# A two-layer diffusion trunk: another clock for the order of the instructions, and part of the modulation on quarters of TensorE's columns

## The chip, the cores and the metric

One core of a Trainium2 chip runs the whole step. The metric is device time in microseconds. The engines are TensorE (PE, with its weight loads PEld), VectorE (DVE), ScalarE (ACT), GpSimd (POOL) and SyncE (SP), which issues the DMAs. All five work through their own instructions in order and wait for each other by semaphores.

## The reference

The trunk has two layers on 128 context tokens and 512 latent tokens of 1024 features. The first mixes by gated linear attention and retention (4 heads each), the second by latent attention (8 heads); each is followed by a squared-ReLU MLP of 4096. Around each sub-layer stand norms, and a modulation that is computed from two condition vectors, c for the latent tokens and c_ctx for the context:

```python
def ada_mod(cond, w_ada, b_ada):
    m = jnp.einsum('bd,de->be', jax.nn.silu(cond), w_ada) + b_ada
    return jnp.split(m[:, None, :], 6, axis=-1)      # shift, scale, gate, shift, scale, gate

def pre_norm_mod(x, g, shift, scale):
    return rms_norm(x, g) * (1.0 + scale) + shift

def post_norm_residual(x, y, g, gate):
    return x + gate * rms_norm(y, g)

# per layer: mixer(pre_norm_mod(x)) -> post_norm_residual, mlp(pre_norm_mod(x)) -> post_norm_residual
# within a tile the gated linear attention needs, for both directions,
#   a = where(causal, (q * exp(b)) @ (k * exp(-b)).T, 0) ; o = q_dec @ S + a @ v
```

w_ada has 1024 rows and 6 x 1024 columns for each layer, 24 MB a layer. All is float32.

## The kernel before

The 640 tokens stand in 5 tiles of 128 (tile 0 the context). Large products take both operands as two summands of a shorter float format, hi and lo, and add three products (`mm3`); ScalarE rounds the weights to hi (`wh`), DVE or POOL subtracts to get lo (`wl`). Small products keep full float32, in two passes.

The program is not written in its final order. Its parts are generators (threads); `Weave` holds a rough clock for each engine, takes each instruction's time from a table in `Engine.way`, and gives out the instructions in the order in which an engine that is free would take them, by priority and then by age. What comes out is a fixed order on each engine. Where the table is off, an engine meets an instruction whose operands are not there yet, and all behind it waits.

The modulation has 12 parts (2 layers, 6 each), each in two halves of 512 columns. A half needs 8 blocks of 128 rows of w_ada (tile `rada`). There are two ways to compute it:
- `ada_first` does shift and scale of the first norm, for which all else waits. PE multiplies each block with a 128 x 4 matrix `wide` that holds both conditions; four of the eight row blocks of scale go to DVE (`FIRST_ON_VECTOR`), whose sums PE adds by columns of ones. The bank's 4 rows are copied to `row` and turned to columns.
- `ada_half` and `ada_cols` do all other parts. DVE multiplies each block by a condition per row and adds, once for each condition (`ada<-rada,cT,ada`, 16 instructions a half), then transposes in blocks of 32 (`tr`) and reduces (`sums`); a PE product with `fold` adds the 4 groups of partitions (`pc`).

The parts of the even layer's gate and of its MLP's shift and scale (`ADA_EVEN`) run during the even layer, the rest in the MLPs. The first projection, `gemm_first`, runs the first group of columns (480) over all tiles with the first half of the features, then with the second, as the first norm's modulation comes by halves. In the even layer `tile_thread` does a tile's work, among it the scores of the two directions: 4 products of 64 rows for the forward direction into one bank, then 4 for the backward one.

Of the kernel before, what the change touches and what calls it, by code (L numbers as in the profile page):

```python
# [35 lines left out]
NCONST = 1320  # L36


def _constants():
# [4 lines left out]
    # running sums of log decays over a tile, taken from its middle (the 1/16 of the gate is in here)  # L44
# [20 lines left out]
    c[:, C_FOLD:] = j % 32 == np.arange(32)  # L65
# [4 lines left out]
# The parts of the kernel are generators that emit instructions; they are interleaved by a rough  # L70
# clock per engine, so that each engine's instructions come in the order in which their operands do.
# [5 lines left out]
class Slots:  # L77
    """The tiles of a tag (or of several pools), handed out and given back."""
# [16 lines left out]
class Weave:  # L95
    """Each thread's instructions come in their order; an engine that is free takes, of those that could start,
    the one of the lowest priority number, then the one that has waited longest (the vector engine: the
    one of the oldest thread)."""
# [14 lines left out]
    # what a thread does between two yields  # L113
    def put(self, *ways):
        """An instruction, in one way or another: engine, time, what emits it."""
        self.cur.todo.append((ways, self.beside))

    def later(self, do):
        """Something for the order itself, behind what the thread has to do so far."""
        if self.running:  # L120
            self.cur.todo.append((((None, 0.0, do),), False))
# [32 lines left out]
    # the order  # L154
# [9 lines left out]
    def _at(self, th, eng):  # L164
        """When what the thread's next instruction needs is there."""
# [6 lines left out]
    def _end(self, th, eng, us):  # L172
        """When that could be through on this engine, behind those that go first."""
# [4 lines left out]
    def _advance(self, th):  # L178
        """To the thread's next instruction, or to what it waits for."""
        while th.todo:  # L180
            ways, beside = th.todo[0]
            if ways[0][0]:
                eng, us, do = ways[0] if len(ways) == 1 else min(ways, key=lambda x: self._end(th, *x[:2]))
                th.todo[0] = us, do, beside
# [25 lines left out]
    def _issue(self, eng, start):  # L210
# [3 lines left out]
        # rather idle for a moment than be in the way of what is more urgent  # L214
# [7 lines left out]
        us, emit, beside = th.todo.popleft()  # L222
        emit()
        if eng == "SP":
# [33 lines left out]
class Engine:  # L258
    """An engine of nc whose instructions also move its rough clock."""
# [4 lines left out]
    def way(self, fn, a, k):  # L264
# [6 lines left out]
        if fn == "dma_start":  # L271
            return "SP", out.shape[0] * n * 4 / 350e3, emit
        if name == "PE":
# [10 lines left out]
            return name, us, emit  # L284
# [3 lines left out]
        psum = any(x.space == bass.MemoryType.PSUM for x in aps)  # L288
        if name == "DVE":
            fast = fn in ("tensor_copy", "tensor_scalar", "memset") and not psum  # L290
            return name, 0.07 + n / (1920 if fast else 960) + 0.06 * small, emit
        if name == "ACT":
            return name, (0.05 if psum else 0.094) + n / 1200 + 0.093 * small, emit
        return name, 0.15 + n * 2.1e-3, emit
# [3 lines left out]


class Either:  # L300
    """Whichever of some engines is through with it first."""
# [20 lines left out]
class Trunk:  # L322
# [31 lines left out]
    def at_last(self, left, do):  # L354
        """do() when the last of left[0] comes here."""
# [11 lines left out]
    def split(self, hi, lo, src, eng=None):  # L367
        """src == hi + lo, both in the tensor engine's one-pass float32 format."""
# [9 lines left out]
    def rsqrt(self, m, r, t, scale, post=1.0):  # L378
        """r = post * (scale * m) ** -0.5, with a Newton step behind exp(-ln / 2)."""
# [13 lines left out]
    def weight(self, src, shape, lo="vector", pair=False, quota=None, room=None, prio=1):  # L393
        """To be brought in as its two summands, in the order of these calls."""
# [4 lines left out]
    def weights(self):  # L399
        """Their loads; weight_rooms() finds room for the summands."""  # L400
# [64 lines left out]
    def gemm_nat(self, units, n, out, ready=None, done=None):  # L465
        """One group of columns, tile by tile of tokens: sets out[t] to the bank."""
# [20 lines left out]
    def gemm_first(self, units, n, out, ready):  # L487
        """The same, all tiles with the first half of the rows, then all with the second."""
# [25 lines left out]
    def ada_loads(self, parts, slots, nk=1, ahead=16, after=None):  # L514
        """The rows of w_ada behind ada_half(), nk * 128 at a time."""
# [16 lines left out]
    def ada_later(self, secs, slots, nk=1, ahead=16):  # L532
        """Loads of whole parts, in their order."""
        self.w.spawn(self.ada_loads([(l, sec, half, k0) for l, sec in secs for half in range(2)
                                     for k0 in range(0, KC, nk)], slots, nk, ahead, self.loaded))

    def ada_half(self, l, sec, half, rest, n=KC):
        """Partial sums over the rows' 128 features of silu(cond) @ w_ada, for both conditions."""
# [1483 lines left out]
```

## Time and profile before

| | us |
|---|---|
| median of 3 runs | 1617.75 |
| lowest, highest | 1616.5, 1625.09 |
| span of the profiled execution | 1615.8 |
| PE busy in it | 1529.0 (95%) |
| DVE, ACT, POOL busy | 1051.6, 634.0, 397.4 |
| mean granted TensorE clock | 0.977 |

The stages in the trace: the first norm and its modulation up to the first projection at 37 us, the even layer to about 410, its MLP to about 845, the latent attention to about 1160, and the second MLP to the end. An instruction shows as busy until its result is out, and those on PE overlap, so the distance of two starts tells the rate, and the busy time of one is longer. The clock of PE is granted in full or in half, in stretches of 3.4 or 6.8 us; a mean of 0.85 over a stage stands for 30% of it at half.

### The profile page before, as it was taken

The page shows a single profiled execution, that of the slowest core. Times are in us where ns is not written, and L with a number is a line of the kernel's source. Part 1 is how long each engine was busy: PE and PEld are TensorE (multiplying, and loading weights), DVE is VectorE, ACT ScalarE, POOL GpSimd, SP SyncE. Part 2 cuts the span into 40 slices and gives each one's busy share as a digit, 9 for nine tenths or more (in the row PEclk, how much of TensorE's full clock was granted, in tenths as well). Part 3 has the DMA queues.
Part 4 walks back from the last instruction along what each step waited for, and adds up shares of the span by engine and source line. Part 5 has one row for each costly group of instructions (what it writes and reads, how often), then busy time and mean ns, then how long its engine had stood idle before and what let it go on. Part 6 is the DMA issues. An engine that isn't in the chain of part 4 may idle for free. (4 is left out here: it accounts for less than half of the span.)

```text
span 1615.8 us, 22873 instructions
## 1 busy us (share of the span) xinstructions
PE 1529.0 (95%) x8583; PEld 1338.8 (83%) x8583; DVE 1051.6 (65%) x1915; ACT 634.0 (39%) x1485; POOL 397.4 (25%) x317
## 2 busy tenths in 40 slices
PE   5999988889999999999997989999899999999997
PEld 1587767777888998998896989998799989988996
DVE  5577898885577778768748788884766333333335
ACT  2473433354532322332235556664543223222332
POOL 2423644432111211211136320012212112111213
PEclk9999999999999999999998999999999999999999
DMA  8323423333265454445322301113344222222211
GB/s 307 106 64 109 121 85 114 102 117 96 73 178 163 143 147 142 137 144 150 116 61 84 97 21 27 40 40 118 104 130 130 72 74 68 90 79 66 78 53 65
DMA packets 146733, 166.12 MB, mean 103 GB/s; under 512 B 12112, under 2 KB 92480, under 8 KB 146624
## 3 DMA queue, kind: packets, MB, share of 16 engines
q1 hardware_dynamic: 146624, 164.68, 33.8%
q8 instruction: 67, 1.10, 0.3%
q14 instruction: 42, 0.34, 0.1%
HBM read 158.69 MB, written 5.96 MB: 102 GB/s over the span
## 5 line engine op out<-in xcount | busy, mean ns | idle before, releaser
L266 PE MATMUL p<-hT,wh 128*128 128x256 f32 (+1 forms) x2048 | 444.3, 309 | 0.0
L266 PE MATMUL p<-wh,hid 128*128 128x512 f32 x1280 | 401.8, 392 | 0.0
L266 PEld LDWEIGHTS p<-hT,wh 128*128 128x128 f32 x2048 | 342.6, 188 | 1.4
L266 PE MATMUL p<-hT,wl 128*128 128x256 f32 (+1 forms) x1024 | 316.6, 309 | 0.0
L266 POOL TENSOR_TENSOR r<-r 128x384 f32<-128x384 f32 (+1 forms) x128 | 133.6, 1044 | 725.8 <-ACT hid L266 725.8
L266 PEld LDWEIGHTS p<-wh,hid 128*128 128x128 f32 x1280 | 241.8, 189 | 49.2
L266 PE MATMUL pg<-wh,hT 128*128 128x512 f32 (+3 forms) x840 | 269.4, 394 | 3.9 <-ACT hT L266 3.5
L266 ACT CAST wh<-raw 128x1024 fp32r<-128x1024 f32 (+3 forms) x169 | 172.3, 1026 | 251.2 <-PE p L266 243.3
L266 PE MATMUL p<-wl,hid 128*128 128x512 f32 x640 | 251.1, 392 | 0.0
L266 DVE SCALAR_TENSOR_TENSOR ada<-rada,cT,ada 128x512 f32<-128x512 f32 x292 | 238.7, 859 | 2.6 <-DMA rada<-in_w_ada 2.4
L266 DVE TENSOR_TENSOR wl<-raw,wh 128x1024 fp32r<-128x1024 f32 x121 | 148.3, 1225 | 89.5 <-ACT wh L266 88.3
L266 PEld LDWEIGHTS p<-hT,wl 128*128 128x128 f32 x1024 | 193.4, 189 | 0.2
L266 PEld LDWEIGHTS pg<-wh,hT 128*128 128x128 f32 x840 | 158.0, 194 | 37.9 <-issue 8.1
L266 DVE TENSOR_TENSOR y<-y,p 128x512 f32<-128x512 f32 x140 | 95.9, 685 | 104.7 <-PE p L266 104.5
L266 DVE TENSOR_TENSOR hid<-r,hid 128x384 fp32r<-128x384 f32 (+1 forms) x128 | 63.9, 500 | 152.6 <-POOL r L266 152.6
L266 ACT ACTIVATE r<-p 128x384 f32<-128x384 f32 (+1 forms) x128 | 56.1, 439 | 266.5 <-PE p L266 266.3
L266 POOL TENSOR_TENSOR wl<-raw,wh 128x1024 fp32r<-128x1024 f32 (+3 forms) x44 | 105.1, 2400 | 211.1 <-ACT wh L266 184.0
L266 PE MATMUL pg<-wl,hT 128*128 128x512 f32 (+3 forms) x360 | 145.8, 405 | 1.1 <-POOL wl L266 1.1
L266 PEld LDWEIGHTS p<-wl,hid 128*128 128x128 f32 x640 | 120.9, 189 | 24.2
L266 PEld LDWEIGHTS pg<-wl,hT 128*128 128x128 f32 x360 | 70.2, 195 | 16.3 <-issue 2.6
L266 ACT ACTIVATE hid<-r 128x384 fp32r<-128x384 f32 (+1 forms) x128 | 60.4, 472 | 2.2
L266 PE MATMUL ps<-kn,qn 128*128 128x320 f32 (+1 forms) x216 | 49.7, 311 | 1.4 <-ACT prob L266 1.4
(259 smaller groups left out, 2013.8 us busy)
## 6 DMA issues: line engine op xcount, KB each, us to landing
raw<-in_w_mlp SPq DMA_DIRECT2D x128, 512.0 KB, 4.2
rada<-in_w_ada SPq DMA_DIRECT2D x160, 256.0 KB, 2.9
rada<-in_w_ada SPq DMA_DIRECT2D x16, 512.0 KB, 5.4
raw<-in_w_in_even SPq DMA_DIRECT2D x16, 512.0 KB, 3.7
x<-in_x_sample SPq DMA_DIRECT2D x8, 512.0 KB, 7.7
gate<-gate SPq DMA_DIRECT2D x8, 512.0 KB, 4.6
raw<-in_w_out_even SPq DMA_DIRECT2D x8, 512.0 KB, 3.9
raw<-in_w_out_odd SPq DMA_DIRECT2D x8, 512.0 KB, 4.2
```

The lines of the kernel that those rows point to most:

```text
L266: emit = lambda: real(*a, **k)
```

## The change

The diff also strips comments and docstrings; those lines are left out here. It has four parts.

1. The order's clock: matmul times are replaced (128 columns of a one-pass product 0.058 in place of 0.108 us, 512 columns 0.2275 in place of 0.216, small float32 products on at most 64 rows more), and a new clock "port" is held by POOL's instructions and by those of DVE that read two operands from SBUF or copy within it: while one holds it the other is not started.
2. The first norm's shift and scale are computed by PE alone. `wide` becomes a 34-column matrix with the conditions in columns 2 and 3; a slice of 32 columns of it is the stationary side. Four blocks of rows are one batch, and block j writes partitions 32 j to 32 j + 31 of the bank. All 128 rows are copied, and a product with `fold`, which is now 128 x 128, adds the four quarters while it turns them to columns.
3. The three parts of `ADA_EVEN` go the same way, two batches a half, with four buffers for their loads in place of two. DVE's accumulators move from the whole kernel's pool to the MLPs'.
4. The scores of both directions go into two banks as one batch of 8 products, the two directions in turn.

```diff
 Engine.way:
             if fn == "transpose":
-                us = 0.108
+                us = 0.08
             elif x.dtype == F32:
-                us = 2 * max(0.108, m * 2 / 2400)
+                us = 2 * max(0.113 if x.shape[0] > 64 else 0.213, m * 2 / 2400)
             else:
-                us = max(0.108, m / 2400 + 0.0025)
+                us = max(0.058, m * 0.4385e-3 + 0.003)
...
+            port = sbuf > 1 or fn in ("tensor_copy", "tensor_scalar") and not psum
...
-        return name, 0.15 + n * 2.1e-3, emit
+        return name, 0.2 + n * (0.6e-3 if fn == "memset" else 2.15e-3), emit, fn != "memset"
 Weave._issue:
+        if port:
+            start = max(start, self.clk.get("port", 0.0))
+            self.clk["port"] = start + us
 new:
+    def batch(self, fn, calls, us):
+        ways = [self.way(fn, a, k) for a, k in calls]
+        self.w.put((self.name, us, lambda: [x[2]() for x in ways], False))
+    def ada_four(self, ps, rows, start, stop):
+        self.nc.tensor.batch("matmul", [
+            ((ps[32 * j:32 * j + 32], self.wide[:, kc, 2 - 2 * sec:34 - 2 * sec], raw), dict(start=start, stop=stop))
+            for j, (raw, kc, sec) in enumerate(rows)], 1.4)
+    def ada_turned(self, ps, n, row):
+        nc.scalar.copy(row, ps)
+        yield
+        for j in range(4):
+            nc.tensor.matmul(ps[:, n * j:n * j + n], row[:, j * P:(j + 1) * P], self.fold[:, 0:n], start=True, stop=True)
+    def ada_tensor(self, l, sec, half, res):
+        ps, hp = yield from self.bank()
+        for k0 in (0, 4):
+            got, held = [], []
+            for kc in range(k0, k0 + 4):
+                raw, hr = yield self.ada_ev[l, sec, half][kc]
+                got.append((raw, kc, 0))
+                held += hr
+            self.ada_four(ps, got, k0 == 0, k0 == 4)
...
 ada:
+            if (l, sec) in ADA_EVEN:
+                yield from self.ada_tensor(l, sec, half, res)
+                continue
 ada_first:
-            n = FIRST_ON_VECTOR[half]
-                w.spawn(by_vector(half, n, done))
-                nc.tensor.matmul(ps[0:4], wide[:, sec * KC + kc], raw, start=(sec, kc) == todo[0],
+            todo = [(k0, sec) for k0 in (0, 4) for sec in (1, 0)]
+            for i, (k0, sec) in enumerate(todo):
...
+                self.ada_four(ps, got, i == 0, i == 3)
 even:
-        self.ada_later(ADA_EVEN, self.slots(ph, "erada", 2))
+        self.ada_later(ADA_EVEN, self.slots(ph, "erada", 4))
 tile_thread:
+            nc.tensor.batch("matmul", [((pas[d][0][:, c], kt[r, c], qt[r, 0, c]), dict(start=True, stop=True))
+                                       for c in cols_ for d, r in enumerate(rows_)], 2.2)
```

PE, the first norm's modulation, before and now. `rada` is a pair of row blocks, `xn` a normed tile that is turned; the first number of the size is the columns of the stationary side.

```order
L266 MATMUL ps_140<-rada_137,wide_114 4x512 x2
L266 MATMUL ps_140<-rada_149,wide_114 4x512
L266 MATMUL ps_140<-rada_146,wide_114 4x512
L266 MATMUL ps_250<-ident,xn_238 128x128
L266 MATMUL ps_140<-rada_149,wide_114 4x512
L266 MATMUL ps_250<-ident,xn_238 128x128
L266 MATMUL ps_140<-rada_146,wide_114 4x512
```

```order
L269 MATMUL ps_134<-rada_137,wide 32x512 x2
L269 MATMUL ps_134<-rada_143,wide 32x512 x2
L269 MATMUL ps_240<-ident,xn_226 128x128 x3
L269 MATMUL ps_134<-rada_140,wide 32x512 x2
L269 MATMUL ps_134<-rada_146,wide 32x512 x2
L269 MATMUL ps_240<-ident,xn_226 128x128
L269 MATMUL ps_134<-fold,row_135 128x4 x4
```

The products of four columns stood one by one between the transposes; now two rows (four products) stand together, and four small products with `fold` follow.

PE, the end of the first half of the first projection (`pg`), now: the first batch of `ADA_EVEN` stands between the halves, where before no modulation of that kind was on PE.

```order
L269 MATMUL ps_553<-ident,xn_313 128x128 x4
L269 MATMUL ps_558<-ident,xn_380 128x128 x4
L269 MATMUL ps_566<-rada_322,wide 32x512
L269 MATMUL ps_566<-rada_330,wide 32x512
L269 MATMUL ps_566<-rada_334,wide 32x512
L269 MATMUL ps_566<-rada_336,wide 32x512
L269 MATMUL pg_337<-wh_360,hT_91 128x480
```

All twelve batches now stand ahead of the first transposes of `dup`, the decayed queries and keys of the retention.

DVE, the rows ahead of the first copy to `dup`, before and now; `ga` is the gate of the linear attention, `sm` small columns of a norm.

```order
L266 SCALAR_TENSOR_TENSOR ada_1519<-rada_1736,cT,ada_1519 128x512
L266 SCALAR_TENSOR_TENSOR ada_1520<-rada_1736,cT,ada_1520 128x512
L266 TENSOR_REDUCE sm_1809<-sq_1808 128x4
L266 TENSOR_SCALAR sm_1809<-sm_1809 128x4
L266 STREAM_TRANSPOSE tr_1857<-ada_1519 128x512
L266 TENSOR_TENSOR sm_1809<-sm_1809 128x4 x2
L266 TENSOR_SCALAR sm_1809<-sm_1809 128x4
L266 TENSOR_TENSOR sm_1809<-sm_1809 128x4
L266 COPY dup_1884<-qk_1873 128x4x64
```

```order
L269 TENSOR_SCALAR sm_1802<-sm_1802 128x4
L269 SCALAR_TENSOR_TENSOR ga_1662<-ps_1752,sm_1751,ga_1662 128x128
L269 TENSOR_TENSOR sm_1766<-sm_1766 128x4
L269 TENSOR_TENSOR ga_1850<-pg_1759,ga_1850 128x512
L269 COPY dup_1905<-qk_1892 128x4x64
```

The multiply-adds and the transpose of the modulation are gone from here.

More of the change, by code (lines that the diff above doesn't have):

```diff
@@ L629, in ada_first @@
         res = [self.mod_tile(sec) for sec in range(2)]
-        wide, hd = yield from self.take(self.tmp, [P, 512], F32, "wide")
-        wide = wide[:, 0:72].rearrange("p (k c) -> p k c", c=4)
-        nc.vector.memset(wide, 0.0)
-        for c in range(2):
-            nc.vector.memset(wide[:, 16 + c, 2 + c:3 + c], 1.0)
+        nc.vector.memset(self.wide, 0.0)
         def load():
@@ L650, in load @@
             w.set(self.loaded)
-        def by_vector(half, n, done):
-            acc = yield from self.ada_half(0, 1, half, 0.0, n)
-            w.set(done, acc)
         w.spawn(load())
         yield prepared
-        for sec in range(2):
-            nc.vector.tensor_copy(wide[:, sec * KC:sec * KC + KC, sec * 2:sec * 2 + 2],
-                                  self.cT.rearrange("p (c k) -> p k c", c=2))
+        nc.vector.tensor_copy(self.wide[:, :, 2:4], self.cT.rearrange("p (c k) -> p k c", c=2))
         for half in range(2):
@@ L663, in ada_first @@
             row, hw = yield from self.take(self.tmp, [P, 512], F32, "row")
-            n = FIRST_ON_VECTOR[half]
-            done = Event()
-            if n:
-                w.spawn(by_vector(half, n, done))
-            todo = [(sec, kc) for kc in range(KC) for sec in range(2) if sec == 0 or kc >= n]
-            for sec, kc in todo:
-                raw, hr = yield self.ada_ev[0, sec, half][kc]
-                nc.tensor.matmul(ps[0:4], wide[:, sec * KC + kc], raw, start=(sec, kc) == todo[0],
-                                 stop=n == 0 and (sec, kc) == todo[-1])
-                self.drop(*hr)
-                yield
-            if n:
-                acc = yield done
-                for c in range(2):
-                    nc.tensor.matmul(ps[0:4], wide[:, 16 + c], acc[c], start=False, stop=c == 1)
-                yield
-            nc.scalar.copy(row[0:4], ps[0:4])
-            for j in range(4):
-                nc.tensor.transpose(ps[:, 4 * j:4 * j + 4], row[0:4, j * P:(j + 1) * P], self.ident[0:4, 0:4])
-            yield
+            todo = [(k0, sec) for k0 in (0, 4) for sec in (1, 0)]
+            for i, (k0, sec) in enumerate(todo):
+                got, held = [], []
+                for kc in range(k0, k0 + 4):
+                    raw, hr = yield self.ada_ev[0, sec, half][kc]
+                    got.append((raw, kc, sec))
+                    held += hr
+                self.ada_four(ps, got, i == 0, i == 3)
+                self.drop(*held)
+                yield
+            yield self.cols_ready
+            yield from self.ada_turned(ps, 4, row)
             pv = ps[:, 0:16].rearrange("p (j s c) -> p s c j", s=2, c=2)
-            yield self.cols_ready
             for sec in range(2):
@@ L791, in run @@
         self.ident = const("ident", [P, P])
-        self.fold = const("fold", [P, 32])
+        self.fold, self.wide = const("fold", [P, P]), const("wide", [P, KC, 34])
         self.cT, self.cols = const("cT", [P, 16]), const("cols", [P, 160])
@@ L885, in main @@
                 load(post[16:32], k_rows("norm_mlp_post")),
-                load(self.fold, io["consts"][:, C_FOLD:C_FOLD + 32]), then=lambda at: w.set(arrived2, None, at))
+                load(self.fold, io["consts"][:, C_FOLD:C_FOLD + P]), then=lambda at: w.set(arrived2, None, at))
         yield arrived
```

57 lines of the change are left out of this document (33 added, 24 removed).

## The prediction

> **What bounds the kernel now.** I read the page first, then a table of stages with the granted clock, then the timeline of the start, then the waits of the even layer.
>
> ```profile
> span 1615.8 us, 22873 instructions
> PE 1529.0 (95%) x8583; PEld 1338.8 (83%) x8583; DVE 1051.6 (65%) x1915; ACT 634.0 (39%) x1485; POOL 397.4 (25%) x317
> rada<-in_w_ada SPq DMA_DIRECT2D x160, 256.0 KB, 2.9
> rada<-in_w_ada SPq DMA_DIRECT2D x16, 512.0 KB, 5.4
> ```
>
> TensorE (PE) is busy for 95% of the span, so an edit can win only PE work or PE standstill. The two other rows are the loads of w_ada, with the median time from issue to landing; they are used below. The table of stages says where PE stands still. Its columns are the stage, its length, busy time and instruction count of PE, its weight loads, VectorE (DVE), ScalarE (ACT) and GpSimd (POOL), then the granted clock.
>
> ```profile
> core 0: us, PE busy (x) PEld busy (x) DVE busy (x) ACT busy (x) POOL busy (x), PEclk, DMA share, GB/s
> 0.00:37.20 37.20, 20.53 (x49) 4.29 (x49) 18.34 (x46) 9.17 (x19) 4.94 (x6) 0.95 0.92 322
> 37.20:61.30 24.10, 23.07 (x59) 6.56 (x59) 12.96 (x29) 8.50 (x17) 13.49 (x10) 0.93 0.42 125
> 61.30:89.70 28.40, 25.87 (x126) 20.80 (x126) 18.48 (x28) 17.31 (x44) 12.13 (x8) 1.00 0.34 98
> 89.00:212.00 123.00, 117.73 (x672) 99.01 (x671) 95.79 (x141) 60.42 (x149) 56.92 (x43) 0.96 0.32 95
> 212.00:235.00 23.00, 16.59 (x80) 13.51 (x79) 19.84 (x47) 6.76 (x18) 6.30 (x6) 0.85 0.28 84
> 235.00:275.00 40.00, 35.44 (x182) 29.25 (x182) 35.30 (x58) 13.12 (x27) 20.83 (x19) 0.91 0.39 112
> 275.00:320.00 45.00, 39.43 (x213) 33.28 (x212) 37.45 (x50) 14.62 (x28) 18.24 (x10) 0.92 0.36 101
> 320.00:360.00 40.00, 35.48 (x175) 28.57 (x174) 35.39 (x59) 21.46 (x43) 13.96 (x6) 0.95 0.39 124
> 360.00:410.00 50.00, 44.31 (x192) 35.45 (x192) 26.03 (x51) 21.20 (x53) 15.08 (x8) 0.91 0.28 86
> 410.00:845.00 435.00, 433.94 (x2477) 394.33 (x2476) 317.37 (x485) 142.15 (x287) 71.32 (x67) 1.00 0.46 134
> 845.00:890.00 45.00, 35.72 (x172) 29.47 (x171) 35.14 (x69) 23.83 (x72) 27.05 (x19) 0.87 0.24 82
> 890.00:1140.00 250.00, 240.74 (x1632) 225.84 (x1631) 186.47 (x544) 149.30 (x456) 50.25 (x40) 1.00 0.18 54
> 1140.00:1160.00 20.00, 14.36 (x60) 11.43 (x59) 13.85 (x23) 8.04 (x19) 8.38 (x4) 0.83 0.41 132
> 1160.00:1615.00 455.00, 446.52 (x2520) 407.60 (x2518) 199.87 (x296) 138.81 (x260) 79.18 (x74) 1.00 0.28 84
> ```
>
> Both MLPs (410 to 845, 1160 to 1615) are dense at full clock: 435 us hold 434 of PE work. Nothing there can shrink by reordering. From 212 to 360, in the even layer, 148 us hold 126.9 us of PE work, so 21.1 are idle; and the clock there, 0.85, 0.91, 0.92 and 0.95, costs 23 x 0.15 + 40 x 0.09 + 45 x 0.08 + 40 x 0.05 = 12.7 us more. From 89 to 212 the same count gives 5.3 idle and 4.9 of clock, and from 360 to 410 it gives 5.7 and 4.5. The start is a third kind: DMA is busy for 0.92 of the first 37 us, and PE waits for it.
>
> **Part one: the first norm's modulation.** Before, 28 products of four columns run one by one on PE (12 and 2 for each half), eight row blocks go to DVE. Now 32 run in eight batches of four, each of a batch on its own quarter of the columns.
>
> ```profile
> 11.06 0.98 SPq L266 DMA_DIRECT2D rada<-in_w_ada  x1
> 17.93 3.48 PE L266 MATMUL ps<-rada,wide 128*4 128x512 f32 x4 [3.21 <-DMA rada<-in_w_ada]
> 25.23 2.74 PE L266 MATMUL ps<-rada,wide 128*4 128x512 f32 x6
> 29.72 0.58 ACT L266 COPY row<-ps 4x512 f32<-4x512 f32 x1 [2.60 <-PE ps L266]
> 31.59 2.53 POOL L266 TENSOR_TENSOR wl<-raw,wh 128x960 fp32r<-128x960 f32 x1 [4.91 <-ACT wh L266]
> 31.97 2.17 DVE L266 SCALAR_TENSOR_TENSOR mod<-mod,cols 128x8 f32<-128x8 f32 x1
> 37.21 0.48 PE L266 MATMUL pg<-wh,hT 128*128 128x480 f32 x1 [3.48 <-ACT hT L266]
> 38.93 5.36 SPq L266 DMA_DIRECT2D rada<-in_w_ada  x4
> 53.70 1.02 PE L266 MATMUL ps<-rada,wide 128*4 128x512 f32 x2
> 54.66 0.49 PE L266 MATMUL pg<-wl,hT 128*128 128x480 f32 x1
> 55.07 1.02 PE L266 MATMUL ps<-rada,wide 128*4 128x512 f32 x2
> ```
>
> A product is two passes. Six passes in 2.74 us, the last with a tail, put them 0.43 us apart. Between 53.70 and 55.07 stand one product (0.86) and one projection matmul (some 0.2: 126 instructions fill 25.87 us from 61.3 on), so 0.3 of the 1.37 goes to changing between the forms. A batch then costs between 2 x 0.43 + 0.3 = 1.16 us, the quarters fully side by side, and 8 x 0.43 + 0.3 = 3.74, one after the other. No row shows quarters at work. I take b = 1.5, nearer the lower end, as the four write different partitions and use different columns. A table of the Trainium skill ("TensorE: Matmul & The Clock Gate", Part 3, Measured speedup vs the span model) gives 2.38 times for three column tiles; used for four it would make b 3.44 / 2.38 + 0.3 = 1.75, and the forecast 5 us later; no run here shows it yet.
>
> Chain of the first half: its last load is issued by 12.04; with the median landing of 5.4 us it is there at 17.4, and if loads queue at the busy share of 0.92, some 3 us later, so at about 20.5. One cold batch (at half clock 2.5), the row copy (0.6) and four small products bring the columns to about 24.5; before, the copy starts at 29.72 and the projection at 37.21, 7.5 later, of which some 2 is the tiny DVE instruction that lasts 2.17 us while POOL's 2.53 us piece runs. So the projection starts at 28 to 30 in place of 37.2: **-8**. In the second half 14 interleaved products of 1.37 - 0.2 = 1.17 (16 us) become four batches of 1.5 (6 us), on a PE that is busy 23.07 of 24.10: **-10**. Against it: the last two loads were issued at 38.93 and DMA was at 0.92 until then. They land earlier only as far as slots free earlier, so PE may stand idle for them around 40: **+4**. Part one gives -14, between -22 (no such wait) and -3 (loads set the pace).
>
> **Part two: gate, shift and scale of the even layer.** These 6 halves leave DVE and become 12 batches on PE, 12 x 1.5 = 18, with 24 small products onto columns, less 6 products with the summing matrix.
>
> ```profile
> L266 DVE SCALAR_TENSOR_TENSOR ada<-rada,cT,ada 128x512 f32<-128x512 f32 x79 | 83.5, 1084 | 2.6 <-DMA rada<-in_w_ada 2.4
> L266 DVE SCALAR_TENSOR_TENSOR ada<-rada,cT,ada x292: 733/746/2899, 6.6 to 1236.0; 128x512 f32<-128x512 f32 x146
> 290.90 10.83 POOL L266 TENSOR_TENSOR wl<-raw,wh 128x1024 fp32r<-128x1024 f32 x4 [19.61 <-PE ps L266]
> 296.60 6.34 DVE L266 SCALAR_TENSOR_TENSOR ada<-rada,cT,ada 128x512 f32<-128x512 f32 x3
> 307.05 0.31 PE L266 MATMUL pc<-sums,fold 128*32 128x32 f32 x2 [5.57 <-DVE sums L266]
> PE ps L266 <- DVE dup L266: 11.0, 2, 6.4
> 122.51 0.71 PE L266 MATMUL ps<-qt,kt 64*128 64x128 f32 x4
> 123.46 0.48 PE L266 MATMUL ps<-qt,kt 64*128 64x128 f32 x2
> L266 PE MATMUL ps<-qt,kt 64*128 64x128 f32 x80 | 20.2, 336 | 0.0
> ```
>
> The product with the sums takes 0.31 for its pair; a small product in a run costs perhaps 0.2 (an estimate, that row less its tail). So 18 + 4.8 - 1.9 = **+21** of PE work. What it buys is the first row: 79 multiply-adds that cost DVE 83.5 us between 80 and 410. Their mean there is 1084 ns where the fastest is 733. The pair of rows at 291 to 303 shows why: three of them last 6.34 us, 2.1 each, while POOL runs weight pieces of 2.7 us back to back. PE then waits 5.57 us, in order, for the sums that they make, and loses full clock behind it. The two waits for the tile dup (11.0 us) are behind the same multiply-adds in DVE's order. Of the 33.7 us lost from 212 to 360 I take 70%, of the 10.2 from 89 to 212 30%, of the 10.2 from 360 to 410 nothing, as that wait is the tail of a norm: 24 + 3 = **-27**, between 0 and -44. Each batch now waits, in PE's order, for four loads; behind it queue the projection's matmuls, and behind those ScalarE's copies of their banks. Before, only DVE waited for them, 2.4 us in all. I cost that at nothing, since the loads have four buffers and as many projection matmuls ahead of them; uncovered, 12 landings of 2.9 us would be 35. Late next, once these are gone, are the small DVE steps behind POOL's pieces, which stay.
>
> **Part three: the scores.** Two more passes add 0.23 to a pair of 0.48, so a pass in a run costs 0.115; eight pairs alone cost 8 x 0.48 = 3.8 us and in one run 0.48 + 14 x 0.115 = 2.1. Five tiles: -8.7 at most, 0 at least; tails overlap with what follows, so **-6**.
>
> **Part four: the order's clock.** It moves rows everywhere, and its price is in no row. The MLPs have no standstill to lose or win. In the odd layer, 845 to 1160, 315 us hold 24.2 of idle and 45 x 0.13 + 20 x 0.17 = 9.3 of clock. An order that knows of the blocked DVE may fill some, one that is new may open others: between -20 and +12, I take **-3**. DVE's work in the MLPs is unchanged; larger constants, a wider row copy and two banks instead of one for the scores cost under 1 us and lie under PE work; without that cover they cost that 1.
>
> **Sum:** -14 + 21 - 27 - 6 - 3 = -29 on the profiled 1615.8, so 1586.8. The median of the runs, 1617.75, lies 1.95 above the span, so about **1589 us**.
>
> **Rivals.**
>
> *The quarters run one after the other.* Nothing in the trace shows them side by side. Then b is 3.74, and 20 batches cost 20 x 2.24 = 45 more than in the sum: 1634, slower. The point from which it decides is b = 1.5 + 28.75 / 20 = 2.9 us.
>
> *POOL keeps the lock.* The stalls stay because DVE's small steps still meet POOL's weight pieces, as the 2.17 us at 31.97 does, which is no multiply-add. Then -27 becomes -5 and the time 1611. The Trainium skill says so too ("SBUF — State Buffer", SBUF: two separate sides): the port pair is an exclusive lock, the loser blocks for the whole instruction; the rows at 31.59 and 31.97 agree. Against this rival: between 80 and 410 the multiply-adds are by far DVE's largest group, and DVE loses that load.
>
> *The loads hold the start.* DMA at 0.92 speaks for it; against it that PE's 16 us of products follow the loads. Part one gives -3: 1600.
>
> *The order finds more.* All 44 us of the stalls' bound, and 20 in the odd layer: 1589 - 17 - 17 = 1555.
>
> **How the numbers follow.** Forecast 0.42; quarters in turn 0.12, with 0.02 for other slowdowns of such size; lock 0.16; loads 0.14; more 0.14. What a measurement of this kernel tells from no change is 0.5%, 8 us. The forecast, the loads, the better order and a little of the lock case (0.02) are faster: 0.72. The rest of the lock case is within 0.5%: 0.14. Slower: 0.14. The range leaves out most of the serial case and some of the best: 1558 to 1618; the forecast's own runs from 1572 (stalls all gone) to 1605 (b of 2.3).
>
> **What would show it.** In the new trace: starts of four quarter passes a few ns apart, and a batch of 1.2 to 1.7 us; the first projection matmul before 31 us; the last of 480 columns near 80, with two to four batches of part two ahead of it, not just before 89.7; no multiply-add on DVE before 400; granted clock above 0.95 from 212 to 360 in place of 0.85 to 0.95; the first MLP's start some 30 us earlier and its length unchanged. Wrong if passes of a batch stand 0.43 us apart, if PE waits for w_ada loads inside the even layer, or if it waits as long as before for dup and y with DVE idle but blocked.

## The result and the profile after

The changed kernel takes 1567.72 us (median of four runs, 1566.1 to 1568.41) against 1617.53 for the kernel before (median of its four runs in the same comparison): a ratio of 0.9676, 95% interval 0.9654 to 0.9697. That is 49.8 us faster. The prediction said 1589 with a range of 1558 to 1618: the direction and the range hold, the gain is 1.7 times the 29 us forecast.

The page of the changed kernel, its span, busy times and the two rows of w_ada's loads:

```profile
span 1565.8 us, 23013 instructions
PE 1508.6 (96%) x8731; PEld 1338.3 (85%) x8731; DVE 939.7 (60%) x1776; ACT 635.0 (41%) x1467; POOL 387.3 (25%) x317
rada<-in_w_ada SPq DMA_DIRECT2D x160, 256.0 KB, 3.4
rada<-in_w_ada SPq DMA_DIRECT2D x16, 512.0 KB, 9.1
```

To see where the 50 us come from, I cut both spans at the same events: first and last projection matmul of 480 columns, first matmul of the first MLP, last matmul of each MLP's second product, first matmul of the second MLP. The table of stages of the kernel before, cut there (columns as in the prediction; the first stages are the start, the projection of 480 columns and the rest of the even layer):

```profile
37.20:89.30 52.10, 48.53 (x181) 27.02 (x182) 31.05 (x57) 25.41 (x60) 25.22 (x18) 0.97 0.38 112
89.30:416.40 327.10, 295.09 (x1530) 243.99 (x1529) 254.87 (x412) 141.50 (x327) 131.02 (x91) 0.93 0.33 99
```

The same of the changed kernel, all six stages:

```profile
0.00:34.90 34.90, 17.64 (x63) 5.29 (x64) 13.15 (x34) 10.67 (x23) 5.85 (x7) 0.84 0.92 326
34.90:79.90 45.00, 42.58 (x219) 28.85 (x218) 13.18 (x38) 24.76 (x58) 21.49 (x17) 0.97 0.55 179
79.90:361.00 281.10, 277.43 (x1629) 230.48 (x1627) 163.63 (x302) 142.35 (x310) 122.28 (x91) 0.99 0.37 113
361.00:813.30 452.30, 451.71 (x2546) 411.88 (x2547) 331.80 (x506) 148.74 (x309) 82.04 (x76) 1.00 0.43 128
813.30:1108.60 295.30, 271.73 (x1764) 252.75 (x1762) 216.96 (x602) 170.32 (x513) 75.11 (x54) 0.95 0.22 67
1108.60:1565.80 457.20, 447.48 (x2517) 409.05 (x2517) 200.97 (x295) 138.17 (x259) 80.49 (x74) 0.99 0.27 82
```

The start is 2.3 us shorter, the projection 7.1, the rest of the even layer 46.0. The first MLP is 9.1 shorter and the odd layer 12.7 longer, which belong together (work moved across the cut): +3.6. The second MLP is 1.8 longer. Sum: -2.3 - 7.1 - 46.0 + 3.6 + 1.8 = -50.0.

In the even layer VectorE (DVE) lost 91 us of work, from 254.87 to 163.63, and TensorE (PE) almost all of its idle time: 327.1 - 295.1 = 32.0 before, 281.1 - 277.4 = 3.7 now. The granted clock went from 0.93 to 0.99. Of the 44.4 us that stand at half clock in the kernel before, PE is busy for 33.5, so the clock costs about 33.5 / 2 = 17 us beside the idle time; now 3.4 us stand at half, all of them busy, which cost 2. Idle time and clock together are 28 + 15 = 43 of the 46 us that the stage lost; by this estimate the other 3 are less work of PE.

The waits of PE in that stage, before and after, of the view of waits:

```profile
PE ps L266 <- DVE dup L266: 11.0, 2, 6.4
PE pc L266 <- DVE sums L266: 8.3, 2, 5.6
PE ps L266 <- DVE y L266: 5.7, 1, 5.7
```

```profile
PE ps L269 <- ACT row L269: 0.7, 1, 0.7
PE ps L269 <- ACT vb L269: 0.4, 1, 0.4
PE ps L269 <- DVE y L269: 0.3, 1, 0.3
```

All three long waits are gone, the one for y at the layer's end among them, which the prediction had left alone.

### The profile page after: what moved, and what is told of

Same layout as the page of the kernel before. It is cut to its first block, busy times and chain, and to the rows that moved or that the text cites. A ratio compares the mean times of both kernels' runs of the same rounds, so it can differ in the third digit from the quotient of the medians.

```text
span 1565.8 us, 23013 instructions
## 1 busy us (share of the span) xinstructions
PE 1508.6 (96%) x8731; PEld 1338.3 (85%) x8731; DVE 939.7 (60%) x1776; ACT 635.0 (41%) x1467; POOL 387.3 (25%) x317
## 4 chain that ended last, share of the span: by engine, by line
PE 89%; DVE 4%; ACT 3%; DMA 1%; issue 1%; POOL 1%; SPq 1%; DVEq 0%; ACTq 0%; POOLq 0%
PE p L269 56%; PE pg L269 18%; PE ps L269 12%; PE pqk L269 2%; DVE sm L269 1%; PE pv L269 1%; ACT junk L269 1%; DVE x L269 1%; DMA x<-in_x_sample 1%; DMA rada<-in_w_ada 1%; SPq L269 1%; DVE y L269 0%; DVE prob L269 0%; ACT h L269 0%; ACT wh L269 0%
## 5 line engine op out<-in xcount | busy, mean ns | idle before, releaser
L269 PE MATMUL p<-hT,wh 128*128 128x256 f32 (+1 forms) x2048 | 450.7, 311 | 4.8 <-ACT hT L269 4.2
L269 PEld LDWEIGHTS p<-hT,wh 128*128 128x128 f32 x2048 | 347.4, 190 | 6.9 <-ACT hT L269 4.7
L269 PEld LDWEIGHTS p<-wh,hid 128*128 128x128 f32 x1280 | 240.3, 188 | 49.6
L269 PE MATMUL pg<-wh,hT 128*128 128x512 f32 (+3 forms) x840 | 265.6, 388 | 0.0
L269 POOL TENSOR_TENSOR wl<-raw,wh 128x1024 fp32r<-128x1024 f32 (+3 forms) x44 | 100.1, 2290 | 217.5 <-ACT wh L269 106.8
L269 DVE SCALAR_TENSOR_TENSOR ada<-rada,cT,ada 128x512 f32<-128x512 f32 x196 | 146.8, 783 | 0.0
L269 PE MATMUL pg<-wl,hT 128*128 128x512 f32 (+3 forms) x360 | 141.6, 393 | 0.0
L269 POOL TENSOR_TENSOR wp<-raw,wp 128x512 fp32r<-128x512 f32 (+1 forms) x18 | 25.2, 1405 | 96.3 <-ACT wp L269 96.3
```

The lines of the kernel that those rows point to most:

```text
L269: emit = lambda: real(*a, **k)
```

## The experiments

Every stage below is cut at the events above; "even" is the rest of the even layer, "later" both MLPs and the odd layer together. Times of stages are of the profiled execution.

| run | median us | ratio to before, 95% | start | projection | even | later |
|---|---|---|---|---|---|---|
| before | 1617.5 | | 37.2 | 52.1 | 327.1 | 1199.4 |
| changed | 1567.7 | 0.9676 (0.9654 to 0.9697) | 34.9 | 45.0 | 281.1 | 1204.8 |
| clock alone | 1617.5 | 0.9994 (0.9984 to 1.0003) | 37.0 | 47.6 | 326.9 | 1203.1 |
| part two alone | 1609.3 | 0.9940 (0.9923 to 0.9957) | 36.7 | 54.4 | 318.9 | 1198.3 |
| scores alone | 1605.4 | 0.9915 (0.9896 to 0.9935) | 36.9 | 53.4 | 316.9 | 1198.8 |
| changed, old clock | 1581.6 | 0.9777 (0.9757 to 0.9796) | 36.2 | 50.1 | 294.2 | 1199.2 |
| changed, no port lock | 1592.0 | 0.9835 (0.9820 to 0.9850) | 35.5 | 50.2 | 299.5 | 1207.2 |
| changed, part two on DVE | 1590.1 | 0.9828 (0.9810 to 0.9847) | 34.2 | 38.1 | 317.0 | 1198.2 |
| changed, scores as before | 1592.5 | 0.9843 (0.9802 to 0.9884) | 35.8 | 45.2 | 314.3 | 1205.8 |
| changed, one quarter | 1609.4 | 0.9945 (0.9925 to 0.9966) | 36.6 | 58.4 | 307.4 | 1203.3 |
| changed, first norm as before | 1574.5 | 0.9730 (0.9712 to 0.9748) | 38.4 | 53.7 | 277.6 | 1205.8 |

### Each part alone, and all without the clock

Theory A: the standstill goes because the multiply-adds leave DVE. Theory B: it goes because the order now knows of the port lock.

The clock alone: the kernel before with the new `way`, the new times and the port in `_issue`.

```diff
+        if port:
+            start = max(start, self.clk.get("port", 0.0))
+            self.clk["port"] = start + us
```

> The kernel before with the new clock of the order alone (matmul times, the port lock, GpSimd's times); the same instructions as before. Theory A (the standstill of the even layer goes because the 96 multiply-adds leave VectorE): the stalls stay, 1600 to 1618 us, first MLP's start within 10 us of before's 416. Theory B (it goes because the order now knows of the port lock and puts VectorE's and GpSimd's work apart): 1570 to 1590, first MLP's start near 375.

Measured: no change, and the even layer as long as before (326.9). These are theory A's numbers, but it is another even layer. The waits for dup are gone, and one new wait stands at its end. PE's waits and its timeline there:

```profile
PE pc L269 <- DVE sums L269: 30.2, 2, 18.8
```

```profile
380.53 0.32 PE L269 MATMUL pc<-sums,fold 128*32 128x32 f32 x2 [11.40 <-DVE sums L269]
399.67 0.31 PE L269 MATMUL pc<-sums,fold 128*32 128x32 f32 x2 [18.82 <-DVE sums L269]
```

From 366 to 400 PE is busy for 3.78 us, while DVE works through the last multiply-adds (27.06 us busy). The new order serves the other work of the layer first and leaves the modulation for last; the gain is given back at the end, to the microsecond.

Part two alone: the kernel before with `ada_tensor` for the even layer's three parts, the old clock, the old first norm and the old scores.

```diff
+            if (l, sec) in ADA_EVEN:
+                yield from self.ada_tensor(l, sec, half, res)
+                continue
```

> The kernel before with the even layer's modulation on quarters of TensorE alone: old clock, old first norm (its sums over rows kept in the room of the later gate rows), old scores. Theory A: most of the 46 us of the even layer, 1572 to 1588. Theory B: 12 to 15 us more of TensorE work partly paid by fewer stalls, 1600 to 1620. If each needs the other: between, about 1595, and the first run near 1600 too.

Measured: 9 us faster (0.9940), within theory B's numbers. The wait for the sums is gone; those for dup (4.4, here released by ScalarE) and y (5.6) stay. And something shows that the kernel before has only in short stretches (below, at the scores alone). Two rows of its table of stages:

```profile
127.00:148.00 21.00, 21.00 (x76) 14.36 (x77) 8.77 (x12) 4.56 (x12) 6.99 (x7) 0.51 0.50 168
158.00:175.00 17.00, 17.00 (x56) 11.27 (x56) 2.19 (x3) 0.43 (x1) 2.54 (x2) 0.50 0.20 64
```

PE is counted busy for all of 38 us, and its granted clock is half. No wait stands there. That costs 19 us, more than what the part gained.

All parts but the clock: the changed kernel with the old `way` and no port.

> The changed kernel with the order's clock of before (batches keep their written prices). Theory A: 1568 to 1582, the even layer's stalls stay away. Theory B: above 1595, stalls for dup and sums back.

Measured: 1581.6, at the upper end of what theory A said, though not all the stalls stay away. So some three quarters of the gain come without the clock, but neither the clock nor part two brings it alone. Without the clock, dup (5.0) and y (5.7) are waited for. Why y is late, from the timeline of this run:

```profile
358.33 7.12 POOL L269 TENSOR_TENSOR wl<-raw,wh 128x1024 fp32r<-128x1024 f32 x3 [28.48 <-ACT wh L269]
358.62 2.13 DVE L269 SCALAR_TENSOR_TENSOR sm<-sm 128x1 f32<-128x1 f32 x1 [0.31 <-ACT sm L269]
360.98 2.15 DVE L269 TENSOR_TENSOR sm<-sm 128x1 f32<-128x1 f32 x1
363.22 3.31 DVE L269 SCALAR_TENSOR_TENSOR x<-y,sm,x 128x1024 f32<-128x1024 f32 x1
370.60 0.66 PE L269 MATMUL ps<-ident,y 128*128 128x128 f32 x2 [5.70 <-DVE y L269]
```

And the same place in the changed kernel:

```profile
354.95 1.23 DVE L269 TENSOR_TENSOR wl<-raw,wh 128x1024 fp32r<-128x1024 f32 x1 [0.79 <-ACT wh L269]
356.09 0.35 DVE L269 SCALAR_TENSOR_TENSOR sm<-sm 128x1 f32<-128x1 f32 x2
357.63 0.41 PE L269 MATMUL ps<-ident,y 128*128 128x128 f32 x2 [0.27 <-DVE y L269]
```

In the old order three of POOL's weight pieces run back to back across the norm's chain, two tiny DVE steps each last nearly as long as a piece, and the step on x behind them takes 3.31 us (1.28 at 357.40 in the changed kernel). (The Trainium skill, "SBUF — State Buffer", SBUF: two separate sides, calls the shared ports an exclusive lock under which the loser blocks for the whole instruction; these rows agree, 2.13 and 2.15 us for steps that take 0.15 to 0.2 elsewhere.) With the lock in the clock, no piece of POOL lies across the last tile's chain.

### Undoing one part of the changed kernel

Part two back on DVE (the whole kernel's pool of SBUF has no room left for the sums, so they lie in the even layer's):

```diff
-            if (l, sec) in ADA_EVEN:
-                yield from self.ada_tensor(l, sec, half, res)
-                continue
-        self.ada_later(ADA_EVEN, self.slots(ph, "erada", 4))
+        self.pada = self.pool(ph, "eada", 1)
+        self.ada_later(ADA_EVEN, self.slots(ph, "erada", 2))
```

> The changed kernel with the even layer's gate, shift and scale back on VectorE (96 multiply-adds, two buffers for the rows of w_ada, the sums in the even stage's own room). The clock alone (the same instructions as before, new order) gained nothing: its first stalls went, and TensorE stood 30 us at the layer's end for the sums. Theory A2 (the new order needs the multiply-adds gone: otherwise the wait moves to the layer's end): that 30 us wait again, 1585 to 1605. Theory B (the order and the batched scores do it): within 8 us of the changed kernel, 1560 to 1576.

Measured: 22 us lost. The wait at the layer's end is there again, and no other of its size:

```profile
PE pc L269 <- DVE sums L269: 34.2, 3, 19.5
```

So this is settled: the new order needs the multiply-adds gone, otherwise it pays with 30 to 34 us of waits for them. Together with the first run this names the interaction. The clock takes away the waits for dup and y, part two the wait for the sums, and either one alone leaves the other's. For part two alone that is the smaller share, though: its even layer is 37.8 us longer than the changed kernel's, 6 of them idle time (10.1 against 3.7) and 23 half clock (49.6 us of it busy against 3.4, halved); the rest is work of PE, the old scores among it.

The scores as before:

```diff
-            nc.tensor.batch("matmul", [((pas[d][0][:, c], kt[r, c], qt[r, 0, c]), dict(start=True, stop=True))
-                                       for c in cols_ for d, r in enumerate(rows_)], 2.2)
             for d, M in ((0, A), (1, B)):
...
+                for h in range(NH):
+                    s = slice(h * P, (h + 1) * P)
+                    nc.tensor.matmul(pa[:, s], kt[r, s], qt[r, 0, s], start=True, stop=True)
```

> The changed kernel with the scores as before, one direction at a time and each product on its own in the order. By the prediction's term (6, at most 8.7): 1574 to 1576. By the times of the passes in the traces (17.4 us before, 5.5 now): 12 us, 1580. If single products also cost TensorE its full clock, as two half-clock stretches of 17 and 20 us at full occupancy in the run with part two alone suggest: 1585 to 1600.

Measured: 25 us lost (1586 to 1603 in four runs, the widest of all), twice what the passes take. There is no long wait. The table of stages shows the rest, in the profiled execution, whose span is 35 us over the changed kernel's:

```profile
110.00:138.00 28.00, 28.00 (x112) 19.45 (x112) 8.84 (x20) 8.79 (x27) 6.28 (x7) 0.51 0.22 75
161.00:176.00 15.00, 15.00 (x56) 11.16 (x56) 1.48 (x3) 1.01 (x2) 1.28 (x1) 0.54 0.30 89
```

Again PE is counted busy throughout at half clock: 28 x 0.49 + 15 x 0.46 = 21 us lost, which with the 12 of the passes is 33 of the 35. The changed kernel has in the same two stretches:

```profile
110.00:138.00 28.00, 27.98 (x218) 21.33 (x218) 15.09 (x22) 13.86 (x35) 15.57 (x15) 1.00 0.68 213
161.00:176.00 15.00, 15.00 (x72) 12.55 (x71) 9.90 (x15) 8.18 (x15) 12.27 (x13) 1.00 0.20 60
```

The scores alone, on the kernel before:

```diff
+            nc.tensor.batch("matmul", [((pas[d][0][:, c], kt[r, c], qt[r, 0, c]), dict(start=True, stop=True))
+                                       for c in cols_ for d, r in enumerate(rows_)], 2.2)
```

> The kernel before with the scores of both directions in one batch, and nothing else. The passes themselves fall from 17.4 to 5.5 us: if they are on the path, 1606. If the time goes to the waits for VectorE behind them, which stay: 1612 to 1618. If they cost full clock as well: 1595 to 1602.

Measured: 12.2 us faster, about the passes' own time, 17.4 - 5.5 = 12 us. That is in part chance: in the even layer PE's busy time falls by 15.1 us (295.1 to 280.0), and its idle time rises by 4.9 (32.0 to 36.9).

Half clock with PE busy all the while, and in the 3.4 us ahead too, stands in the kernel before as well:

```profile
109.92:113.33 3.41, 3.41 (x15) 2.76 (x13) 2.16 (x8) 0.59 (x1) 0.00 (x0) 0.50 0.09 10
126.99:133.82 6.83, 6.83 (x24) 5.58 (x24) 6.79 (x9) 2.19 (x6) 4.60 (x4) 0.50 0.58 199
```

All four traces whose scores are single products have such stretches: two in the kernel before, one with the clock alone (6.8 us at 119.7), three each in the two runs that also have the even layer's quarter batches, up to 20.5 and 27.3 us long. Ahead of each of the nine, the last 3.4 us hold 6 to 9 single passes of the scores. Of the traces with the scores in batches only the one on a single quarter (below) has one, 6.8 us at 105.3, behind eight passes of its sums over 32 rows. So the half clock goes with the single scores, and is long where the quarter batches stand beside them. Single scores are not enough for it: from 136 to 162 the kernel before has them at full clock. What in the mixture brings the clock down wasn't separated.

The clock without the lock: matmul and POOL times new, no port.

```diff
-        if port:
+        if port and False:
```

> The changed kernel whose order knows the new matmul and GpSimd times but not the port lock. If the lock is what the new clock gains by (the old clock in full costs 14 us): 1577 to 1585. If the matmul times are: 1565 to 1572.

Measured: 1592.0, 24 us lost, and 10 us worse than with the old clock in full. Waits of PE in its even layer:

```profile
PE ps L269 <- DVE dup L269: 6.0, 1, 6.0
PE ps L269 <- DVE y L269: 5.6, 1, 5.6
```

So the new clock gains nothing without the lock (the lock with the old matmul times was not run). Against the changed kernel 18 us of the loss lie in the even layer, where these two waits are back. With the old clock in full they are as long (5.0 and 5.7): of the 12.9 us between these two profiled executions 8.0 lie in "later" and 5.3 in the even layer, and why the new times alone are worse than the old isn't shown.

The first norm as before, its sums kept in the room of the later gate rows:

```diff
+FIRST_ON_VECTOR = (4, 4)
...
-                self.ada_four(ps, got, i == 0, i == 3)
+                nc.tensor.matmul(ps[0:4], wide[:, sec * KC + kc], raw, start=(sec, kc) == todo[0],
+                                 stop=n == 0 and (sec, kc) == todo[-1])
```

> The changed kernel with the first norm's modulation as before: 28 products of four columns on TensorE and eight row blocks on VectorE (whose sums lie in the room of the later gate rows). By the prediction's term: 14 us, 1582. By the stages of the changed kernel (first projection 2.3 us earlier, projection stage 7.1 us shorter): 9 us, 1577. If its 14 late products and two late loads also push the twelve batches of the even layer into the scores' time, as in the run with part two alone: 1590 or more.

Measured: 6.8 us lost (9.7 between the profiled executions). The start is 3.5 longer and the projection 8.7, but the even layer behind it is 3.5 shorter.

### What a batch costs

All four products of a batch on the first quarter; `way` prices products on 32 rows so that the order of all engines stays the same:

```diff
...
-            ((ps[32 * j:32 * j + 32], self.wide[:, kc, 2 - 2 * sec:34 - 2 * sec], raw), dict(start=start, stop=stop))
+            ((ps[0:32], self.wide[:, kc, 2 - 2 * sec:34 - 2 * sec], raw), dict(start=start and j == 0, stop=stop and j == 3))
...
-        nc.scalar.copy(row, ps)
+        nc.scalar.copy(row[0:32], ps[0:32])
...
```

> The changed kernel with all four products of a batch on the first quarter of the columns, so that they add up there one after the other; the sum over quarters then takes 32 rows. The order of every engine is the same. A batch of 8 passes then takes 8 x 0.43 = 3.4 us in place of 1.0: twelve batches of the even layer 29 us, the eight of the first norm up to 19, part of which hides behind the loads: 1600 to 1615. If the passes were not side by side in the changed kernel but only short: no change, 1566 to 1570.

Measured: 41.7 us lost. Batches in the timelines of the changed kernel, then of this run (the columns are start, length to the end of the last pass, then the operation; the next row's start gives what a batch costs):

```profile
97.45 1.06 PE L269 MATMUL ps<-rada,wide 128*32 128x512 f32 x8
98.44 0.38 PE L269 MATMUL ps<-pos,la 128*128 128x2 f32 x2
```

```profile
116.76 3.62 PE L269 MATMUL ps<-rada,wide 128*32 128x512 f32 x8
```

A batch costs 1.0 us on four quarters and 3.55 on one (median of the batches that stand alone, to the next matmul's start). Over the 17 such batches that is 61.3 us against 25.9: 35 of the 40 us between the profiled executions. The rest isn't placed; the sums over 32 rows are a form of their own, with changes of form around it. The first three batches stand together at the start and take 12.6 us against 11.7, hidden behind the loads. The records' starts within a batch, in ns after the one before:

```
four quarters: 7, 6, 7, 433, 7, 8, 5, then 523 to the next matmul
one quarter:   454, 429, 429, 429, 429, 430, 429, then 522
```

Where their loads are there, the four run fully side by side. The matmul ahead of a batch takes about 0.1 us longer to the next start than in a run (0.21 in place of 0.12 ahead of 105.06), so that a batch adds some 1.1 to PE's time. Four of the even layer's twelve in the changed kernel also wait for loads of w_ada between their products, which the view of waits doesn't show since PE counts as busy. They take 2.96 (at 66.7), 1.53 (118.4), 2.53 and 1.19 us (140.6), 4.2 beyond the 1.0 of each; the third is

```profile
126.24 2.60 PE L269 MATMUL ps<-rada,wide 128*32 128x512 f32 x8
```

The directions in turn, in the scores' batch:

```diff
-                                       for c in cols_ for d, r in enumerate(rows_)], 2.2)
+                                       for d, r in enumerate(rows_) for c in cols_], 2.2)
```

> The changed kernel with the same batch of scores, but first all four products of the one direction, then all of the other, in place of one by one; nothing else moves. If 1.09 us for 16 passes comes from the two row halves working side by side, a batch then takes 16 x 0.11 = 1.8 us: five batches 3.5 us more, 1571. If it comes from the run alone (no change between forms): 1.1 us a batch, 1567 to 1568.

Rows of the changed kernel, then of this one:

```profile
98.98 1.16 PE L269 MATMUL ps<-qt,kt 64*128 64x128 f32 x16
100.07 0.38 PE L269 MATMUL ps<-pos,la 128*128 128x2 f32 x2
```

```profile
99.25 1.71 PE L269 MATMUL ps<-qt,kt 64*128 64x128 f32 x16
100.89 0.38 PE L269 MATMUL ps<-pos,la 128*128 128x2 f32 x2
```

A batch takes 1.09 us alternating and 1.64 in turn. Five batches give 2.7 us, and the median is 1568.15, a ratio of 0.9681 (0.9665 to 0.9697): that can't be told from the changed kernel. The rows decide, not the time: alternating products start in pairs 7 ns apart, with 105 ns between pairs, so the two row halves work side by side.

### Two tries for a better version

The new clock loses some 5 us in "later" against the old one. With the old clock from the first MLP on (`way` looks at a flag that `mlp` sets):

> The changed kernel whose order goes by the clock of before from the first MLP on. In the changed kernel both MLPs and the odd layer together take 1204.8 us, with the old clock 1199.1: if the new clock's gain is all in the even layer, 5 us less, 1562. If the layers' order depends on where the even layer ends more than on the clock: 1566 to 1572.

Measured: 1566.29, ratio 0.9680 (0.9663 to 0.9697). The second MLP gains 2.2 us, the first MLP and the odd layer take 748.8 in place of 747.6. No difference from the changed kernel that can be measured.

With DVE making the low summands of the first projection's weights as well:

```diff
+        self.u_in_even = (self.nat_units(io["w_in_even"][0], EVEN_GROUPS[:1], "vector", prio=0)
+                          + self.nat_units(io["w_in_even"][0], EVEN_GROUPS[1:], "gpsimd", prio=0))
```

> The kernel with the old clock from the first MLP on, and the low summands of the first projection's weights (four pieces of 960 columns) made by VectorE instead of GpSimd. At the start VectorE's tiny steps last 1.87 and 1.82 us beside two of GpSimd's pieces, and a copy of 0.74 lasts 1.51. If these hold the projection's start: it comes 2 to 4 us earlier and the whole 2 to 4 us shorter. If the loads hold it: within 1 us of the run before it.

Measured: 1567.63, ratio 0.9685 (0.9669 to 0.9701), no difference from the run before it. What it was meant to remove, in the changed kernel's timeline:

```profile
24.97 2.21 POOL L269 TENSOR_TENSOR wl<-raw,wh 128x960 fp32r<-128x960 f32 x1 [24.53 <-DMA rada<-in_w_ada]
25.32 1.87 DVE L269 SCALAR_TENSOR_TENSOR sm<-sm 128x1 f32<-128x1 f32 x1
27.30 0.17 DVE L269 SCALAR_TENSOR_TENSOR mod<-mod,cols 128x8 f32<-128x8 f32 x1
32.25 1.26 POOL L269 TENSOR_TENSOR hT<-h,hT 128x512 fp32r<-128x512 f32 x1
34.94 0.75 PE L269 MATMUL pg<-wh,hT 128*128 128x480 f32 x1
```

And the run without POOL's pieces there:

```profile
25.06 1.16 DVE L275 TENSOR_TENSOR wl<-raw,wh 128x960 fp32r<-128x960 f32 x1 [1.21 <-DMA rada<-in_w_ada]
26.14 0.21 DVE L275 SCALAR_TENSOR_TENSOR sm<-sm 128x1 f32<-128x1 f32 x1
31.02 3.75 POOL L275 TENSOR_TENSOR hT<-h,hT 128x512 fp32r<-128x512 f32 x2 [30.58 <-ACT hT L275]
32.44 1.94 PE L275 MATMUL ps<-rada,wide 128*32 128x512 f32 x8
34.30 0.77 PE L275 MATMUL pg<-wh,hT 128*128 128x480 f32 x1
```

The tiny step is short again (0.21), but now the first of POOL's two steps on hT lasts 2.5 us, beside a piece of DVE's, where one took 1.26 in the changed kernel: the lock is paid on the other side. And the first product stands in PE's order behind a batch at half clock (32.44), which ends only then. The start gains 1.0 us against the run before and the projection loses 3.2.

## Why the prediction was right, and where its terms were off

**What bounds the kernel.** Right. The MLPs gave nothing, the gain lies in PE's standstill and clock in the even layer, and a little in the start.

**A batch, b = 1.5.** Too dear: it is 1.0 to the next start, 1.1 with the matmul ahead of it, near the lower end of 1.16. The quarters are fully side by side, so nothing had to be added to that end. Of its 0.3 for the change of forms, 0.1 is in the batch's last pass (523 ns, of which 429 are the pass) and about 0.1 in the matmul ahead. Twenty batches at 1.1 are 8 us less than in the sum. (The table of the Trainium skill, "TensorE: Matmul & The Clock Gate", Part 3, Measured speedup vs the span model, has 2.38 times for three column tiles and no row for four; the estimate of 1.75 from it was too dear, as four make 3.55 / 1.0, some 3.6 times, here. The few ns for each further tile that the same section gives, about 4, are near what the records show here, 5 to 8.)

**Part one, -14.** Right in sign, too large: 6.8 for the whole kernel when undone, though 3.5 + 8.7 = 12 at the end of the projection. The failing step is the start, -8: the first projection matmul comes at 34.9, not at 28 to 30. The loads take 9.1 us to land, not 5.4, but the queueing that the chain added covers it: the first half's last one is there at 20.95 (forecast 20.5), and the products that turn the columns end at 25.1 (24.5). What fails is the stretch from there to the projection, put at 4 to 6 and measured 9.8. The chain assumed that the tiny DVE step of 2.17 us behind POOL's piece would not be on it any more; one of 1.87 is (25.32, above), so that the modulation is ready at 27.5, and a second of 1.82 follows at 30.49. In PE's order the transposes of two further tiles stand ahead of the first product, the last of which wait for xn until 34.2. The load wait of +4 around 40 did not come.

**Part two, +21 of work and -27 of stalls.** The work was off by b, 12 x 0.4 = 5 less, and by the batches' wait for loads, put at nothing and measured 4. The stalls were mis-sized: I took 70% of what was lost from 212 to 360, 30% of what was lost ahead of it and none of the wait for y. Idle time and clock together gave 43, nearly all of what the even layer lost. (The bound of 44 counted half clock over idle time as well, 11 of the stage's 44.4 us at half.) What the working missed is that these stalls have more than one owner. The sums' wait belongs to the multiply-adds; the waits for dup and y belong to POOL's pieces across DVE's small steps, and go only with the lock in the clock; part of the half clock goes with the single scores. By the runs, part two without the clock and the batched scores is worth 9 us.

**Part three, -6, at most -8.7.** The bound was wrong. It priced 16 passes one after the other at 0.115; the two directions use different row halves and run side by side, so a batch is 1.09 (1.64 in turn), not 2.1, and the term is -12. Alone, the edit gave 12.2; undone in the changed kernel it cost 25, with the half clock.

**Part four, the order's clock, -3.** The later layers, which the term was about, became 5.4 us longer (-3 forecast, within its -20 to +12). The clock's gain lies where no term of mine looked, in the even layer: 13.9 us for the whole kernel when undone, of which 13.1 in that layer, 5.1 in the projection and 1.3 in the start, less 5.6 later.

**The sum.** The single losses when one part is undone are 6.8 + 22.3 + 24.7 + 13.9 = 68, the single gains where a part was tried alone 0, 9 and 12. The whole is 50. A sum of independent terms could not have given this. That the range holds the time is in part luck: the stalls (43 against 27), b (8 us) and the scores (6) were taken too low, and against them stand a start that came 6 us short and later layers that lost 5 where 3 were to be gained.

**The rivals.** The quarters in turn: refuted, and its price about right (45 worked out, 41.7 measured when forced). POOL keeps the lock: half right. DVE's small steps are blocked as before, but PE no longer stands behind them; without the lock in the order the waits for dup and y do stay. The loads hold the start: its price came true, 6 of the 8 us did not come, but not for its reason, as the last load was there about when forecast. The order finds more: the nearest, 1555 against 1567.7, and for its reason in the even layer; the 20 us in the odd layer did not come. The measured time lies 4 us below the forecast's own range, whose lower end of 1572 (stalls all gone) had kept b and the scores too dear.

**What would show it.** Starts a few ns apart: yes. A batch of 1.2 to 1.7: 1.0. First projection before 31: no, 34.9. Last of 480 columns near 80: 79.9. No multiply-add on DVE before 400: the first is at 395.9, the next stage's. Clock above 0.95 from 212 to 360: 1.00. First MLP some 30 us earlier: 55. Of the signs of being wrong, one came: PE waits for w_ada loads inside the even layer, within the batches, but for 2.3 us there, the rest in the projection.

**Open.** Why the clock falls to half at full occupancy among single scores, and why for so long beside quarter batches; how much of the start is the norm's chain and how much PE's order ahead of the first product, since taking the lock's blocks away moved it by 1 us only; why the new matmul times without the lock are worse than the old.

## What to carry to other kernels

When an order is fixed by a planner, look who owns each stall before summing: here the clock alone gave nothing and the offload alone 9 us, because each removed one loss and another stood next, behind the clock the wait for the sums, behind the offload mostly the half clock. A planner's clock that is corrected in part can be worse than one that is wrong throughout: new matmul times without the port lock cost 10 us against the old clock in full. Small fp32 products are worth packing on different column quarters or row halves of TensorE and issuing as one run, even where each alone looks cheap.

## What the hardware showed that I had not expected

- Four products of 512 columns on the four column quarters start 5 to 8 ns apart and cost about as much as one: 1.0 us for eight passes, against 3.55 on one quarter and 0.95 for a single product of two passes in the kernel before.
- Products on rows 0 to 63 and on rows 64 to 127 run side by side when they alternate: 1.09 us for 16 passes, 1.64 in turn. As single pairs among other forms the same 16 passes took 17.4 / 5 = 3.5 us.
- TensorE can be granted half its clock for 14 to 27 us while it is counted busy all the time: 0.51 over 28.00 us busy of 28.00, and 0.50 over 17.00 of 17.00. In nine of the ten such stretches of these traces, the short ones included, single products on 64 rows stand in the 3.4 us ahead. The Trainium skill ("TensorE: Matmul & The Clock Gate", Part 1, What's actually happening) has the clock follow how busy the array has been of late. The busy share of the profile is then not that measure, since here it was full.
- The lock between VectorE and GpSimd costs whoever comes second: moving four pieces from GpSimd to VectorE shortened VectorE's tiny step from 1.87 to 0.21 us and made a step of GpSimd last 2.5 in place of 1.26.
